# Block sums of weights formed by accumulating loads in a two-layer trunk kernel, with first pairs of a block loaded ahead

## The chip, the cores and the metric

The kernel runs on one core of a Trainium2 chip. The metric is the device time of one execution in microseconds, the median over several runs; lower is better. One execution was profiled by the hardware profiler, and the rows quoted below come from its trace.

## The reference, cut to what matters

Two residual layers act on x (512 tokens, 1024 features). Layer 0 mixes by a gated short convolution and a gated linear recurrence, layer 1 by stick-breaking attention; each is followed by a squared-ReLU MLP with 4096 hidden features, which is where the change lies. All modulation vectors come from `c_act @ ada_w[layer]`.

```python
for layer in range(2):
    mod = c_act @ ada_w[layer] + ada_b[layer]          # ada_w: (2, 1024, 6144)
    shift1, scale1, gate1, shift2, scale2, gate2 = split(mod, 6)
    h = rms_norm(x, norm_mix[layer]) * (1 + scale1) + shift1
    x = x + gate1 * mixer(h)
    h = rms_norm(x, norm_mlp[layer]) * (1 + scale2) + shift2
    x = x + gate2 * (square(relu(h @ mlp_w1[layer])) @ mlp_w2[layer])
```

## The kernel before

**Precision.** Each product of float32 matrices is made from three matmuls (`mm3`, L278): the high part of the weight times the high and the low part of the data, and the low part of the weight times the high part of the data. A weight tile of 128 x 1024 is loaded by SyncE's queue into a ring of three raw buffers (`raw_w`, L258), ScalarE casts it to its high part (`whi`, L271), VectorE subtracts that to get the low part (`wlo`, L272), into rings of four (`split_w`). Hidden tiles are split in the same way (`split`, L288; low parts at L291).

**The MLP** (`mlp`, L1127) makes the 32 hidden tiles of 128 features in four blocks of eight. After each block the second weight matrix is applied to it: outputs o = 0 to 7, eight k steps of 3 matmuls of 512 columns each, added onto x by `x_add` (L506). Block 3 does five outputs there and leaves the last three to the next stage.

**Pairs.** Most hidden tiles are made two at a time, as a 2 x 2 block product of halves (the weights A11, A12 of one tile and A21, A22 of the other; the data's halves of features and of tokens) with seven products of half size instead of eight (Winograd's form of Strassen's scheme), each of 4 k steps x 3 matmuls = 12 matmuls of 256 columns. `pair_w` (L1047) makes the left-hand sums on VectorE into `tt`, which has four places of 1024 columns: S1 = A21 + A22 (L1058), S2 = S1 − A11 (L1059), S4 = A12 − S2 (L1061), S3 = A11 − A21 (L1062). The splits are wa (A11, A12), wb (S1, S2), wc (S4, S3) and wd (A22). `pair` (L1068) runs the products in the order wa, wb, wb, wa, wc, wc, wd; the last, `last()`, runs behind the first products of the next pair. `sums` (L1007) makes the right-hand sums t0 to t3 (high and low parts) once for each layer, from the normalised tiles of h that also stand in `tt`; so `tt` is free for the first pair's sums only after the last low part (L1021) is made. Each raw load of 512 KB goes by SyncE; there are 13 pairs in each layer: pair 3 of block 0 and four in each of blocks 1 to 3.

**Block 0** differs: its first four tiles are made as a head (`mlp_head`, L1177 for layer 0; L1657 to L1672 for layer 1) in two halves of tokens, by k steps, as h becomes ready, each half with four psum banks; tiles 4 and 5 are then made whole (`whole_tile`, L1117), and tiles 6 and 7 are pair 3.

**Background.** In layer 0 `background(2)` after each output of blocks 0 to 2 issues two loads of the ada weights of layer 1 (48 in these blocks), through the same ring of raw buffers and the same queue; VectorE makes their dot products with c (L420).

**Order.** In the MLP only TensorE's order is as written by hand. The orders of SyncE, ScalarE, VectorE and GpSimd follow from the order of emission in the program, through the tile scheduler. The head of layer 1 is placed by a planner (`Graph`), which has costs and due times for its steps and TensorE's order as given. GpSimd has hardly any work in the kernel.

Of the kernel before, what the change touches and what calls it, by code (L numbers as in the profile page):

```python
# [23 lines left out]
P = 128  # L24
# [196 lines left out]
def trunk(tc, x_d, c_d, rep_d, small_d, const_d, ada_d, ws_d, win_d, wv_d, woab_d, w1_d, w2_d, wqk_d, wvc_d, woc_d, out_d):  # L221
# [63 lines left out]
    def ks(k):  # L285
        return slice(k * P, (k + 1) * P)
# [720 lines left out]
    def sums(l, th, on):  # L1007


        lo_, hi_ = slice(0, 4), slice(4, 8)  # L1010
        q = lambda k, hf: tt3[:, k, H[hf]]
        regs = lambda k, hf: [(i, hf) for i in range(k.start, k.stop)]
        s2, hd = l * 48 + SHIFT2 * 8, Handle()
        on("DVE", 8, lambda: dve.tensor_tensor(dsh[:, 4 * l:4 * l + 4], modc[:, s2 + 4:s2 + 8], modc[:, s2:s2 + 4], op=ALU.subtract), [], [hd])
        view = lambda t_: t_.rearrange("p (k t) -> p k t", t=256)

        def high(i, k, hf):
            on("ACT", 1024, lambda: act.copy(view(th[i][0].t), q(k, hf)), regs(k, hf), [th[i][0]])

        def low(i, k, hf):  # L1020
            on("DVE", 1024, lambda: dve.tensor_tensor(view(th[i][1].t), q(k, hf), view(th[i][0].t).bitcast(F32), op=ALU.subtract),  # L1021
               regs(k, hf) + [th[i][0]], [th[i][1]])
# [24 lines left out]
    def pair_w(l, i, hp):  # L1047


        r0, r1 = raw_w(w1_d[l, 2 * i]), raw_w(w1_d[l, 2 * i + 1])  # L1050
        a, b = slice(0, T), slice(T, 2 * T)

        def place():
            nsum[0] += 1
            n = (nsum[0] - 1) % 4
            return tt[:, 1024 * n:1024 * n + 1024]
        wa, s_ = split_w(r0, None, AT256), place()
        dve.tensor_tensor(s_[:, a], r1[:, a], r1[:, b], op=ALU.add)  # L1058
        dve.tensor_tensor(s_[:, b], s_[:, a], r0[:, a], op=ALU.subtract)  # L1059
        wb, z_ = split_w(s_, None, AT256), place()  # L1060
        dve.tensor_tensor(z_[:, a], r0[:, b], s_[:, b], op=ALU.subtract)  # L1061
        dve.tensor_tensor(z_[:, b], r0[:, a], r1[:, a], op=ALU.subtract)  # L1062
        wc = split_w(z_, None, AT256)
        wd = [hp.tile([P, 576], F32R, name=n, tag=n)[:, 16:528] for n in ("wdh", "wdl")]
        split(r1[:, b], *wd)
        return wa, wb, wc, wd

    def pair(l, i, hp, th, hid, before):  # L1068


        wa, wb, wc, wd = pair_w(l, i, hp)
        a, b, c = [acc(256) for _ in range(3)]
        cm = [hp.tile([P, T], F32, name="cm", tag="cm", bufs=3) for _ in range(2)]
        out = [hid_new(hp, 2 * i + j) for j in range(2)]
# [14 lines left out]

        def relu2(j, sl, ps=None):  # L1090
            c_ = cm[j][:, sl]
            act.activation(c_, c_ if ps is None else ps, AF.Relu)
            act.activation(c_, c_, AF.Square)
            split(cm[j], *out[j], sl)

# [18 lines left out]
            relu2(1, H[0], a)  # L1114
        return last

    def whole_tile(l, j, hp, hid):  # L1117

        w, ps, c_ = load_w(w1_d[l, j]), acc(), hp.tile([P, T], F32, name="cm", tag="cm", bufs=3)
# [4 lines left out]
        act.activation(c_, c_, AF.Square)  # L1124
        split(c_, *hid[j])

    def mlp(l, last, hp, head, th):  # L1127
# [49 lines left out]
    def mlp_head(l, nin, hp):  # L1177
# [2 lines left out]
        later(TN, lambda: nin.finish(acc(256), 1))  # L1180
        hid = [hid_new(hp, j) for j in range(4)]

        def head(hf):
            ps = [acc(256) for _ in range(4)]
            for k in range(NT):
                for j in range(4):
                    mm3(ps[j], w[j], ks(k), hT[k], H[hf], k == 0, k == NT - 1)
                yield 1.28
            for j in range(4):
                c_ = hp.tile([P, T], F32, name="cm", tag="cm", bufs=3)  # L1190
                act.activation(c_[:, H[hf]], ps[j], AF.Relu)
                act.activation(c_[:, H[hf]], c_[:, H[hf]], AF.Square)
                split(c_, *hid[j], H[hf])

        run(head(0))
# [136 lines left out]
    def mm3h(ps, cut, w, wc, hs_, hs, start, stop, n, **kw):  # L1332

        h = hs_[0]
        def fn():
            mm3(cut(ps.t), (w[0].t, w[1].t), wc, (h[0].t, h[1].t), hs, start, stop)
        return on_pe(3 * (n * 0.000417 + 0.002), fn, w + tuple(a for h_ in hs_ for a in h_), (ps,), 1, **kw)


# [316 lines left out]

    w = [weights(w1_d[1, j], None, AT256) for j in range(4)]  # L1657
    for hf, sl in enumerate(H):
        ps = [r.new() for r in (accs, accs, zts, miscs)]
        for k, j in by_half(hf, 4):  # L1660
            order.append(mm3h(ps[j], half, w[j], ks(k), (hh[hf][k],), sl, k == 0, k == NT - 1, 256))
        for j in range(4):
            c_, (hi, lo) = cms.new(), hid[j]
            on_act(256, lambda c_=c_, p_=ps[j], sl=sl: act.activation(c_.t[:, sl], half(p_.t), AF.Relu), (ps[j],), (c_,), 0, psum=True)
# [91 lines left out]
```

## Time and profile before

| what | value |
|---|---|
| median of 3 runs | 1263.33 us (fastest 1261.52; a third run of 2425.68 lies far off) |
| profiled execution | 1267.05 us |
| its span in the trace | 1265.3 us |
| granted clock of TensorE, mean | 0.985 |
| DMA | 163.50 MB, mean 129 GB/s |

In the rows below, PE is TensorE's matmuls, PEld its weight loads, DVE VectorE, ACT ScalarE, POOL GpSimd, SP SyncE (SPq its DMA queue). L281 is line 281 of the kernel. In a matmul `b` is the psum bank. A wait row names the engine and line that waited, what it waited for, the total in microseconds, the number of times and the longest. A group row ends with busy time, mean nanoseconds of one, idle time ahead and what ended it. In a DMA row stand the queue, the count, the KB of each and the median time from issue to landing.

### The profile page before, as it was taken

The numbers are of one execution on the slowest core, as the hardware profiler recorded it, in microseconds if no ns is written. First come the engines' busy times: TensorE is split into PE (matmuls) and PEld (weight loads), VectorE is DVE, ScalarE is ACT, GpSimd is POOL, SyncE is SP. The second block draws the span as 40 slices with busy tenths as digits, with TensorE's granted clock in tenths as the row PEclk, the third lists the DMA queues.
The fourth block names the chain that finished last, engine by engine and source line by source line (L and its number), as shares of the span: only waits on it lengthen the run. The fifth ranks groups of instructions, "written<-read, shape, count | busy, mean of one in ns | idle before, by whom it ended". The sixth has DMA issues, their size and how long they took to land.

```text
span 1265.3 us, 19233 instructions
## 1 busy us (share of the span) xinstructions
PE 1227.5 (97%) x7649; PEld 1066.8 (84%) x7649; DVE 891.7 (70%) x1435; ACT 616.7 (49%) x1111; POOL 13.8 (1%) x24
## 2 busy tenths in 40 slices
PE   7999999989999989999999999999989999999998
PEld 6888777888889889889978787778888898898998
DVE  8997777658788687786567764668786574675661
ACT  4433133337338247157357763667565274372560
POOL 0000000000000000000030000000000000000000
PEclk8999899999999989999999999999999999999999
DMA  8666454312764745744312212231113323143141
GB/s 305 252 209 213 161 167 133 133 35 64 250 203 135 253 145 171 253 143 134 107 53 92 84 51 83 85 100 68 51 50 101 100 87 131 67 149 102 51 151 50
DMA packets 46618, 163.50 MB, mean 129 GB/s; under 512 B 5296, under 2 KB 6328, under 8 KB 46528
## 3 DMA queue, kind: packets, MB, share of 16 engines
q1 hardware_dynamic: 46384, 161.78, 38.5%
q8 instruction: 60, 0.98, 0.3%
q10 hardware_dynamic: 144, 0.49, 0.1%
q14 instruction: 30, 0.25, 0.1%
HBM read 155.96 MB, written 2.10 MB: 125 GB/s over the span
## 4 chain that ended last, share of the span: by engine, by line
PE 73%; DVE 10%; DMA 10%; ACT 4%; issue 2%; SPq 0%; ACTq 0%; DVEq 0%
PE b L281 16%; PE b L283 16%; PE b L282 16%; DMA wraw<-in_w 6%; DVE wlo L272 4%; DMA wraw<-in_ada 3%; PE acc L281 3%; PE acc L283 3%; PE acc L282 3%; ACT whi L271 2%; PE acc L652 2%; PE b L1495 1%; PE b L1516 1%; PE b L1551 1%; PE b L1415 1%
## 5 line engine op out<-in xcount | busy, mean ns | idle before, releaser
L271 ACT CAST whi<-wraw 128x1024 fp32r<-128x1024 f32 x125 | 129.7, 1048 | 243.1 <-DMA wraw<-in_w 102.5
L282 PE MATMUL b<-hidl,whi 128*128 128x512 f32 (+1 forms) x560 | 208.3, 372 | 1.5 <-DVE hidl L291 1.5
L281 PE MATMUL b<-hidh,whi 128*128 128x512 f32 (+1 forms) x560 | 208.4, 372 | 0.0
L283 PE MATMUL b<-hidh,wlo 128*128 128x512 f32 (+1 forms) x560 | 207.8, 371 | 0.0
L281 PE MATMUL b<-hh,whi 128*128 128x256 f32 (+1 forms) x632 | 197.7, 313 | 7.0 <-DVE x L506 6.3
L272 DVE TENSOR_TENSOR wlo<-wraw,whi 128x1024 fp32r<-128x1024 f32 x125 | 152.1, 1222 | 62.9 <-ACT whi L271 61.4
L283 PE MATMUL b<-hh,wlo 128*128 128x256 f32 (+1 forms) x632 | 193.2, 306 | 2.3 <-DVE wlo L272 2.3
L282 PE MATMUL b<-hl,whi 128*128 128x256 f32 (+1 forms) x632 | 192.8, 305 | 0.0
L281 PEld LDWEIGHTS b<-hh,whi 128*128 128x128 f32 x632 | 121.1, 192 | 20.1 <-issue 7.2
L506 DVE SCALAR_TENSOR_TENSOR x<-b,modc,x 128x512 f32<-128x512 f32 (+1 forms) x102 | 68.1, 675 | 88.6 <-PE b L283 88.5
L283 PEld LDWEIGHTS b<-hh,wlo 128*128 128x128 f32 x632 | 120.7, 191 | 8.6 <-DVE wlo L272 3.2
L282 PEld LDWEIGHTS b<-hl,whi 128*128 128x128 f32 x632 | 121.3, 192 | 4.5
L282 PEld LDWEIGHTS b<-hidl,whi 128*128 128x128 f32 x560 | 105.5, 188 | 20.7 <-DVE hidl L291 2.8
L283 PEld LDWEIGHTS b<-hidh,wlo 128*128 128x128 f32 x560 | 105.1, 188 | 18.5
L281 PEld LDWEIGHTS b<-hidh,whi 128*128 128x128 f32 x560 | 105.1, 188 | 18.3
L420 DVE CUSTOM_DVE_ANT_0 ascr<-wraw,cb 128x1024 bf16<-128x1024 f32 x80 | 97.8, 1222 | 31.0 <-DMA wraw<-in_ada 30.8
L272 DVE TENSOR_TENSOR wlo<-tt,whi 128x1024 fp32r<-128x1024 f32 x52 | 63.5, 1222 | 19.7 <-ACT whi L271 19.0
L271 ACT CAST whi<-tt 128x1024 fp32r<-128x1024 f32 x52 | 53.2, 1049 | 41.5 <-PE b L282 25.3
L291 DVE TENSOR_TENSOR hidl<-cm,hidh 128x256 fp32r<-128x256 f32 (+1 forms) x90 | 44.5, 510 | 20.1 <-ACT hidh L290 19.3
L1329 DVE TENSOR_TENSOR wlo<-raw,whi 128x1024 fp32r<-128x1024 f32 x34 | 41.5, 1221 | 21.9 <-ACT whi L1328 21.6
L281 PE MATMUL acc<-hh,whi 128*128 128x512 f32 x128 | 52.9, 414 | 0.0
L1479 DVE TENSOR_TENSOR_SCAN om<-om,pat 128x772 f32<-128x772 f32 (+2 forms) x24 | 46.5, 1936 | 5.8 <-ACT om L1475 5.8
(378 smaller groups left out, 2654.2 us busy)
## 6 DMA issues: line engine op xcount, KB each, us to landing
wraw<-in_w SPq DMA_DIRECT2D x124, 512.0 KB, 3.6
wraw<-in_ada SPq DMA_DIRECT2D x80, 512.0 KB, 4.3
eraw<-in_ada SPq DMA_DIRECT2D x16, 512.0 KB, 3.8
wraw<-in_win SPq DMA_DIRECT2D x16, 512.0 KB, 4.1
raw<-in_wqk SPq DMA_DIRECT2D x16, 512.0 KB, 3.7
raw<-in_ws SPq DMA_DIRECT2D x8, 512.0 KB, 6.0
wraw<-in_woab SPq DMA_DIRECT2D x8, 512.0 KB, 3.3
raw<-in_wvc SPq DMA_DIRECT2D x8, 512.0 KB, 3.2
```

The costliest lines, as they stand in the source:

```text
L271: act.copy(hi, raw)
L272: dve.tensor_tensor(lo, raw, hi.bitcast(F32), op=ALU.subtract)
L281: pe.matmul(ps, whi, h[0][:, hs], start=start, stop=False, **kw)
L282: pe.matmul(ps, whi, h[1][:, hs], start=False, stop=False, **kw)
L283: pe.matmul(ps, wlo, h[0][:, hs], start=False, stop=stop, **kw)
L291: dve.tensor_tensor(lo[:, sl], t_[:, sl], hi[:, sl].bitcast(F32), op=ALU.subtract)
L420: dve.tensor_tensor_reduce(out=scr, in0=raw, in1=cb, scale=1.0, scalar=0.0, op0=ALU.mult, op1=ALU.add, accum_out=modr[:, col:col + 1])
L506: dve.scalar_tensor_tensor(x[o][:, sl], ps, mcol(l, v, o), x[o][:, sl], op0=ALU.mult, op1=ALU.add)
L652: order.append(on("PE", 8 * 0.000417 * (sl.stop - sl.start), lambda k=k, wi=wi, hi_=hi_, sl=sl, w=w: [pe.matmul(sacc[j][:, sl], w[wi].t[:, ...
L1329: on_dve(1024, lambda: dve.tensor_tensor(lo.t, raw.t, hi.t.bitcast(F32), op=ALU.subtract), (raw, hi), (lo,), 1)
L1415: on_pe(0.13, lambda s=s, sq=sqs[p, s, s0]: pe.matmul(ms.t[64 + 32 * s:96 + 32 * s, sl], hs, sq.t[:, sl], start=True, stop=True), (sqs[p, ...
L1479: on_dve(2 * nw, lambda: dve.tensor_tensor_scan(s_(), s_(), pats[i][:, ::-1], 0.0, op0=ALU.mult, op1=ALU.max), (om,), (om,), 2)
```

## The change

The signs are chosen so that each left-hand sum is an addition. Two of the four are then formed by a load of one operand by SyncE into `tt`, and a second load, of the other operand, by GpSimd's queue with `accum_op=add` onto the first (which must wait until the first has landed): S1 = A21 + A22 as before, and S3' = A21 + A11. VectorE keeps S2' = S1 + A11 and S4' = A12 + S2'. A22 is loaded once more by itself for wd (256 KB). The operands' signs are carried by a scale of ±1 in the casts and subtractions of the right-hand sums, and row 2 of the pair, which comes out negated, by a scale of −1 in its first ReLU. A pair's loads are now four by SyncE (512, 256, 256 and 256 KB) and two by GpSimd (256 KB each), 1.75 MB in place of 1 MB in two loads.

Beside that:

- `pair_w` is a generator in three steps. In blocks 0 to 2, when output 6 is reached, output 7's weights and the first two steps of the next block's first pair (wa, wb) are emitted ahead of output 6's products, and the third step (wc, wd) ahead of output 7's.
- Background loads stand in `PIECES`: 14, 12, 12 and 10 in blocks 0 to 3, all behind outputs 0 to 4, instead of 16, 16, 16 and none behind outputs 0 to 7.
- In the head of layer 0 the first half of tokens uses two banks, each for two tiles, and the second half is made tile by tile; the weights of tiles 4 and 5 are loaded behind the first two of these, and the right-hand sums are emitted behind the second. The head of layer 1 uses two banks for the first half and four others for the second.

```diff
     def sums(l, th, on):
...
         def high(i, k, hf):
-            on("ACT", 1024, lambda: act.copy(view(th[i][0].t), q(k, hf)), regs(k, hf), [th[i][0]])
+            on("ACT", 1024, lambda: act.activation(view(th[i][0].t), q(k, hf), AF.Copy, scale=1.0 if i == 2 else -1.0), regs(k, hf), [th[i][0]])
 
         def low(i, k, hf):
-            on("DVE", 1024, lambda: dve.tensor_tensor(view(th[i][1].t), q(k, hf), view(th[i][0].t).bitcast(F32), op=ALU.subtract),
-               regs(k, hf) + [th[i][0]], [th[i][1]])
+            on("DVE", 1024, lambda: dve.scalar_tensor_tensor(view(th[i][1].t), q(k, hf), 1.0 if i == 2 else -1.0,
+               view(th[i][0].t).bitcast(F32), op0=ALU.mult, op1=ALU.subtract), regs(k, hf) + [th[i][0]], [th[i][1]])
...
     def pair_w(l, i, hp):
-        r0, r1 = raw_w(w1_d[l, 2 * i]), raw_w(w1_d[l, 2 * i + 1])
         a, b = slice(0, T), slice(T, 2 * T)
+        a11, a21, a22 = w1_d[l, 2 * i][:, a], w1_d[l, 2 * i + 1][:, a], w1_d[l, 2 * i + 1][:, b]
...
-        wa, s_ = split_w(r0, None, AT256), place()
-        dve.tensor_tensor(s_[:, a], r1[:, a], r1[:, b], op=ALU.add)
-        dve.tensor_tensor(s_[:, b], s_[:, a], r0[:, a], op=ALU.subtract)
-        wb, z_ = split_w(s_, None, AT256), place()
-        dve.tensor_tensor(z_[:, a], r0[:, b], s_[:, b], op=ALU.subtract)
-        dve.tensor_tensor(z_[:, b], r0[:, a], r1[:, a], op=ALU.subtract)
-        wc = split_w(z_, None, AT256)
-        wd = [hp.tile([P, 576], F32R, name=n, tag=n)[:, 16:528] for n in ("wdh", "wdl")]
-        split(r1[:, b], *wd)
-        return wa, wb, wc, wd
-
-    def pair(l, i, hp, th, hid, before):
-        wa, wb, wc, wd = pair_w(l, i, hp)
+        def added(out, one, other):
+            sync.dma_start(out, one)
+            pool_e.dma_start(out, other, accum_op=ALU.add)
+        r0 = raw_w(w1_d[l, 2 * i])
+        s_ = place()
+        added(s_[:, a], a21, a22)
+        w = [split_w(r0, None, AT256)]
+        yield w
+        z_ = place()
+        added(z_[:, b], a21, a11)
+        dve.tensor_tensor(s_[:, b], s_[:, a], r0[:, a], op=ALU.add)
+        w.append(split_w(s_, None, AT256))
+        yield w
+        dve.tensor_tensor(z_[:, a], r0[:, b], s_[:, b], op=ALU.add)
+        r1 = wp.tile([P, 1024], F32, name="wraw", tag="raw", bufs=3)[:, :T]
+        sync.dma_start(r1, a22)
+        w.append(split_w(z_, None, AT256))
+        w.append([hp.tile([P, 576], F32R, name=n, tag=n)[:, 16:528] for n in ("wdh", "wdl")])
+        split(r1, *w[3])
+        yield w
+
+    def pair(i, hp, th, hid, before, steps_):
+        for w in steps_:
+            pass
+        wa, wb, wc, wd = w
...
-            act.activation(c_, c_ if ps is None else ps, AF.Relu)
+            act.activation(c_, c_ if ps is None else ps, AF.Relu, scale=1.0 - 2 * j)
...
+    PIECES = ((3, 3, 3, 3, 2), (3, 3, 2, 2, 2), (3, 3, 2, 2, 2), (2, 2, 2, 2, 2))
...
+    def mlp(l, last, hp, head, th, more=()):
...
-                for j in (4, 5):
-                    whole_tile(l, j, hp, hid)
+                for n, j in enumerate((4, 5)):
+                    whole_tile(more[n] if more else load_w(w1_d[l, j]), j, hp, hid)
             for i in range(len(hid) // 2, 4):
-                rest = pair(l, 4 * b + i, hp, th, hid, rest)
+                rest = pair(4 * b + i, hp, th, hid, rest, ahead or pair_w(l, 4 * b + i, hp))
+                ahead = None
...
-                if b < 3:
-                    background(2)
+                if o < 5:
+                    background(PIECES[b][o])
...
             for o in range(2, n):
-                p = second(o)
+                p = p1 if o == n - 1 and b < 3 else second(o)
+                if o == n - 2 and b < 3:
+
+                    p1, ahead = second(n - 1), pair_w(l, 4 * b + 4, hp)
+                    next(ahead)
+                    next(ahead)
                 products(p, 0, 8)
                 done(o, p[0])
+                if o == n - 2 and b < 3:
+                    w = next(ahead)
+                    ahead = [w]
...
-        def head(hf):
-            ps = [acc(256) for _ in range(4)]
...
+        def first():
+            ps = [acc() for _ in range(2)]
+            ps = [ps[j // 2][:, H[j % 2]] for j in range(4)]
             for k in range(NT):
                 for j in range(4):
-                    mm3(ps[j], w[j], ks(k), hT[k], H[hf], k == 0, k == NT - 1)
+                    mm3(ps[j], w[j], ks(k), hT[k], H[0], k == 0 and j % 2 == 0, k == NT - 1, skip_group_check=True)
                 yield 1.28
...
+        def second(j):
+            ps = acc(256)
+            for k in range(NT):
+                mm3(ps, w[j], ks(k), hT[k], H[1], k == 0, k == NT - 1)
+                yield 0.32
+            evict(j, ps, H[1])
+
+        run(first())
         flush()
-        th = [[Handle(t=hp.tile([P, 1088], F32R, name=f"t{i}{a}", tag=f"t{i}{a}")[:, AT512]) for a in "hl"] for i in range(4)]
-        sums(l, th, lambda eng, n, fn, r, w: fn())
-        run(head(1))
-        return hid, [(a.t, b.t) for a, b in th]
+        more = []
+        for j in range(4):
+            run(second(j))
+            if j < 2:
+                more.append(load_w(w1_d[l, 4 + j]))
+            if j == 1:
+                th = [[Handle(t=hp.tile([P, 1088], F32R, name=f"t{i}{a}", tag=f"t{i}{a}")[:, AT512]) for a in "hl"] for i in range(4)]
+                sums(l, th, lambda eng, n, fn, r, w: fn())
+        return hid, [(a.t, b.t) for a, b in th], more
...
     w = [weights(w1_d[1, j], None, AT256) for j in range(4)]
     for hf, sl in enumerate(H):
-        ps = [r.new() for r in (accs, accs, zts, miscs)]
+        ps = [accs.new() for _ in range(2)] if hf == 0 else [zts.new() for _ in range(4)]
+        ps = [(ps[j // 2], lambda t_, j=j: t_[:, H[j % 2]]) if hf == 0 else (ps[j], half) for j in range(4)]
```

More of the change, by code (lines that the diff above doesn't have):

```diff
@@ L1115, in pair, with whole_tile @@
         return last
-    def whole_tile(l, j, hp, hid):
-        w, ps, c_ = load_w(w1_d[l, j]), acc(), hp.tile([P, T], F32, name="cm", tag="cm", bufs=3)
+    def whole_tile(w, j, hp, hid):
+        ps, c_ = acc(), hp.tile([P, T], F32, name="cm", tag="cm", bufs=3)
         for k in range(NT):
@@ L1132, in mlp @@
             if b == 0:
[L1133 to L1134 removed]
+                for n, j in enumerate((4, 5)):
+                    whole_tile(more[n] if more else load_w(w1_d[l, j]), j, hp, hid)
             for i in range(len(hid) // 2, 4):
[L1136 removed]
+                rest = pair(4 * b + i, hp, th, hid, rest, ahead or pair_w(l, 4 * b + i, hp))
+                ahead = None
             n = 8 if b < 3 else 5
@@ L1181, in mlp_head, with evict @@
         hid = [hid_new(hp, j) for j in range(4)]
-        def head(hf):
-            ps = [acc(256) for _ in range(4)]
+        def evict(j, ps, sl):
+            c_ = hp.tile([P, T], F32, name="cm", tag="cm", bufs=3)
+            act.activation(c_[:, sl], ps, AF.Relu)
+            act.activation(c_[:, sl], c_[:, sl], AF.Square)
+            split(c_, *hid[j], sl)
+        def first():
+            ps = [acc() for _ in range(2)]
+            ps = [ps[j // 2][:, H[j % 2]] for j in range(4)]
             for k in range(NT):
                 for j in range(4):
-                    mm3(ps[j], w[j], ks(k), hT[k], H[hf], k == 0, k == NT - 1)
+                    mm3(ps[j], w[j], ks(k), hT[k], H[0], k == 0 and j % 2 == 0, k == NT - 1, skip_group_check=True)
                 yield 1.28
             for j in range(4):
[L1190 to L1195, printed above, removed]
-        flush()
-        th = [[Handle(t=hp.tile([P, 1088], F32R, name=f"t{i}{a}", tag=f"t{i}{a}")[:, AT512]) for a in "hl"] for i in range(4)]
-        sums(l, th, lambda eng, n, fn, r, w: fn())
-        run(head(1))
-        return hid, [(a.t, b.t) for a, b in th]
+                evict(j, ps[j], H[0])
+        def second(j):
[5 more added lines that the diff above has]
+        run(first())
+        flush()
+        more = []
[7 more added lines that the diff above has]
+        return hid, [(a.t, b.t) for a, b in th], more
     m_s = ExitStack()
@@ L1335, in fn @@
         def fn():
-            mm3(cut(ps.t), (w[0].t, w[1].t), wc, (h[0].t, h[1].t), hs, start, stop)
+            mm3(cut(ps.t), (w[0].t, w[1].t), wc, (h[0].t, h[1].t), hs, start, stop, skip_group_check=True)
         return on_pe(3 * (n * 0.000417 + 0.002), fn, w + tuple(a for h_ in hs_ for a in h_), (ps,), 1, **kw)
@@ L1658, in trunk @@
     for hf, sl in enumerate(H):
-        ps = [r.new() for r in (accs, accs, zts, miscs)]
+        ps = [accs.new() for _ in range(2)] if hf == 0 else [zts.new() for _ in range(4)]
+        ps = [(ps[j // 2], lambda t_, j=j: t_[:, H[j % 2]]) if hf == 0 else (ps[j], half) for j in range(4)]
         for k, j in by_half(hf, 4):
-            order.append(mm3h(ps[j], half, w[j], ks(k), (hh[hf][k],), sl, k == 0, k == NT - 1, 256))
+            order.append(mm3h(*ps[j], w[j], ks(k), (hh[hf][k],), sl, k == 0 and (hf == 1 or j % 2 == 0), k == NT - 1, 256))
         for j in range(4):
-            c_, (hi, lo) = cms.new(), hid[j]
-            on_act(256, lambda c_=c_, p_=ps[j], sl=sl: act.activation(c_.t[:, sl], half(p_.t), AF.Relu), (ps[j],), (c_,), 0, psum=True)
+            c_, (hi, lo), (p_, cut) = cms.new(), hid[j], ps[j]
+            on_act(256, lambda c_=c_, p_=p_, cut=cut, sl=sl: act.activation(c_.t[:, sl], cut(p_.t), AF.Relu), (p_,), (c_,), 0, psum=True)
             on_act(256, lambda c_=c_, sl=sl: act.activation(c_.t[:, sl], c_.t[:, sl], AF.Square), (c_,), (c_,), 0)
```

1 line of the change is left out of this document (removed).

## The prediction

> **What bounds the kernel now.** I read the page's busy shares first, then the windows of like stages in the two layers against each other, then the waits of TensorE in the stretch where the windows differ.
>
> ```profile
> PE 1227.5 (97%) x7649; PEld 1066.8 (84%) x7649; DVE 891.7 (70%) x1435; ACT 616.7 (49%) x1111; POOL 13.8 (1%) x24
> ```
>
> TensorE is busy for 97% of the span, so only time that it waits, or runs at half clock after a wait, can be won; VectorE has 30% to spare. The windows (columns: microseconds, then busy time and count of PE, PEld, DVE, ACT, POOL, granted clock, DMA share, GB/s) show where. The first three rows are the four-pair stages that open blocks 1 to 3 of layer 0, the fourth is the same work in layer 1:
>
> ```profile
> 368.10:407.90 39.80, 38.08 (x326) 37.23 (x326) 35.92 (x55) 29.25 (x55) 0.00 (x0) 1.00 0.37 124
> 453.60:498.70 45.10, 41.69 (x326) 41.08 (x325) 39.01 (x59) 30.08 (x57) 0.00 (x0) 0.92 0.35 121
> 544.40:586.80 42.40, 39.25 (x326) 38.64 (x325) 37.73 (x57) 30.93 (x58) 0.00 (x0) 0.96 0.33 114
> 1011.20:1049.40 38.20, 38.20 (x326) 38.19 (x325) 29.26 (x44) 29.14 (x55) 0.00 (x0) 1.00 0.29 99
> 301.10:313.20 12.10, 12.10 (x46) 9.87 (x47) 8.79 (x14) 7.86 (x13) 0.00 (x0) 0.86 0.35 107
> 946.70:957.60 10.90, 10.90 (x51) 9.01 (x50) 10.65 (x15) 6.72 (x13) 0.00 (x0) 1.00 0.37 109
> ```
>
> In layer 1 PE is busy for 38.20 of 38.20 us, with DVE at 29.26: nothing to win there. In layer 0 the same stages take 39.8, 45.1 and 42.4, together 12.7 us more than three times 38.2. The last two rows are whole tiles 4 and 5 of block 0 in layer 0 and in layer 1: 12.1 against 10.9, at a clock of 0.86. The waits of PE in layer 0's MLP say what it stood for:
>
> ```profile
> PE b L281 <- ACT whi L271: 4.7, 3, 2.2
> PE b L283 <- DVE wlo L272: 4.6, 6, 1.7
> PE b L281 <- DVE x L506: 3.2, 1, 3.2
> PE b L282 <- DVE hidl L291: 1.5, 3, 1.1
> ```
>
> Weights that come late head the list; then one wait for the banks of the last x_add (the head), and one for hidden tiles, which this change leaves alone.
>
> **The change, part by part.**
>
> **(1) First pairs prepared ahead.** The timeline row (start, duration, instruction, wait) of the second product of a block's first pair:
>
> ```profile
> 458.07 0.38 PE L281 MATMUL b<-t0h,whi 128*128 128x256 f32 x1 [2.20 <-ACT whi L271]
> 1040.88 0.28 PE L281 MATMUL b<-t0h,whi 128*128 128x256 f32 x1
> ```
>
> Layer 0 waits 2.2 us for wb, whose sums queue on DVE behind the background's dot products; layer 1 doesn't wait. Emitting the loads and splits of wa and wb before output 6's products gives them two outputs, 11 us, of lead. I book all **−12.7**: the clock loss in it has no other cause. What wc and wd need comes before output 7's products, 5.5 us plus two products ahead.
>
> **(2) Whole tiles loaded inside the head.** Wait and slow clock go together:
>
> ```profile
> 301.09 0.50 PE L283 MATMUL b<-hh,wlo 128*128 128x512 f32 x1 [1.67 <-DVE wlo L272]
> ```
>
> 1.67 plus 12.1 − 10.9 = **−2.9**. The loads move ahead of the sums, and the sums after two of four columns.
>
> **(3) Head by two banks.** The first half needs two free banks where four were needed, so the 3.2 us for x_add goes. But the fourth weight's low half is late next, in both layers:
>
> ```profile
> 273.95 1.21 DVE L272 TENSOR_TENSOR wlo<-wraw,whi 128x1024 fp32r<-128x1024 f32 x1
> 922.61 1.22 DVE L1329 TENSOR_TENSOR wlo<-raw,whi 128x1024 fp32r<-128x1024 f32 x1
> ```
>
> The head started at 274.08, and this operand lands at 275.16; in layer 1 at 923.83. The wait only changes its name. I book three short matmuls brought forward, 3 x 0.116 in each layer: **−0.7** (a product of 12 takes 1.39, the time between the start of a pair, 957.60 above, and its second product, 958.99 below). Bounds: 0, and all 3.2 in each, −6.4.
>
> **(4) Background loads bunched.** Before, two ada loads follow each of eight outputs; afterwards all stand behind outputs 0 to 4. Output 5's weight load thus has 14 ada loads of its block ahead of it in block 0, and 12 in blocks 1 and 2, where it had 10. The queue in these stages:
>
> ```profile
> wraw<-in_ada SPq DMA_DIRECT2D x13, 512.0 KB, 4.5
> wraw<-in_w SPq DMA_DIRECT2D x9, 512.0 KB, 4.3
> ```
>
> ```profile
> 407.90:453.60 45.70, 45.47 (x206) 37.38 (x205) 31.85 (x51) 11.48 (x16) 0.00 (x0) 1.00 0.77 254
> ```
>
> 22 loads in 45.7 us through a ring of three buffers are 2.08 each; so output 5's load comes 4 x 2.08 = 8.3 later in block 0 and 4.2 in blocks 1 and 2. Output 5 starts three outputs of (45.7 − 1.4)/8 = 5.54 before the stage's end: 453.6 − 16.6 = 437.0, and at 351.5 in block 0 (which ends where the next stage starts, 368.1); its low half is wanted two matmuls of 0.23 later. It was ready at the ends of these:
>
> ```profile
> 434.13 1.22 DVE L272 TENSOR_TENSOR wlo<-wraw,whi 128x1024 fp32r<-128x1024 f32 x1 [2.25 <-ACT whi L271]
> 346.74 1.23 DVE L272 TENSOR_TENSOR wlo<-wraw,whi 128x1024 fp32r<-128x1024 f32 x1 [1.03 <-ACT whi L271]
> ```
>
> Slack is 437.45 − 435.35 = 2.1 and 351.95 − 347.97 = 4.0. New waits: 2.1 in block 1, the same taken for block 2, and 4.3 in block 0: **+8.5**. Bounds: 0, where the ring was fed late by its consumers and not by its loads, and +16.6, the shift with no slack.
>
> Block 3 carries ten ada loads that it hadn't; its stage has the room that blocks 0 to 2 lose (48 either way).
>
> In the row at 301.09 a wait of 1.67 us was followed by a stage at clock 0.86, so each of these waits may cost 1.2 more; I leave these 3.6 in the range. The Trainium skill's page "TensorE: Matmul & The Clock Gate", section "What's actually happening", has the clock drop after an idle window of about 3.4 us; by that only the 4.3 could cost clock. The row with 1.67 disagrees, and the measurement decides.
>
> **(5) Sums by a second load.** Each of 26 pairs loses two subtractions or additions on DVE:
>
> ```profile
> L1058 DVE TENSOR_TENSOR tt<-wraw 128x512 f32<-128x512 f32 x12 | 8.2, 686 | 0.9 <-DMA wraw<-in_w 0.8
> ```
>
> 52 x 0.69 = 36 us of DVE, worth nothing by itself, since PE in layer 1 waits for none of it. The signs moved into relu's scale and into the sums' casts and subtractions go into instructions that exist: nothing. The loads grow from 1 to 1.75 MB a pair; DMA is at 0.29 to 0.37 in these stages, so bytes aren't the limit. Delay is: S1 is no longer load, 0.69, but load, then POOL's wait for its landing, then a second transfer, in series, of a kind of which no trace here has one. Call that A, from the end of POOL's wait to landing. Bounds from rows of 256 KB:
>
> ```profile
> stq<-stq SPq DMA_DIRECT2D x16, 256.0 KB, 3.4
> ...
> x<-in_x SPq DMA_DIRECT2D x8, 256.0 KB, 4.1
> ...
> out_y<-x SPq DMA_DIRECT2D x5, 256.0 KB, 2.0
> ```
>
> At least 2.0; at most the two slow ones in series, 7.5, since it reads both operands. I take **5**, near the middle, the nearest row being a plain load at 4.1; a plain 256 KB load I take as 3.0, between 2.0 and 4.1.
>
> The Trainium skill's page "DMA: Bandwidth & Descriptors", section "Anatomy of one DMA — SWDGE (gpsimd) path", gives some 2.0 us plus bytes at 436 GB/s, an estimate of 2.6 for A; no run here shows it. By it the waits of the next paragraph vanish and the time would be about 1255.5; by my 5 they stay.
>
> Where it bites first is pair 3 of block 0, whose places in tt are still read by the last right-hand sums:
>
> ```profile
> 948.14 1.22 DVE L1021 TENSOR_TENSOR t2l<-tt,t2h 128x1024 fp32r<-128x1024 f32 x1
> 958.99 0.28 PE L281 MATMUL b<-t0h,whi 128*128 128x256 f32 x1
> ```
>
> ```profile
> 297.55 1.22 DVE L1021 TENSOR_TENSOR t2l<-tt,t2h 128x1024 fp32r<-128x1024 f32 x1
> ```
>
> Free at 949.36, then 3.0 + 5 + 0.69 + cast 1.05 + subtraction 1.22 = 960.3; wanted two matmuls after 958.99, 959.2: wait 1.1. In layer 0 the sums come one column (24 x 0.116 = 2.8) later, free at about 301.8, so 312.8, wanted 301.09 − 1.67 + 10.9 + 1.39 + 0.24 = 312.0: wait 0.8. Together **+1.9**; at A = 2.0 nothing, at 7.5 +6.9.
>
> The steady pairs: SP's next loads wait on z_a as now, and there the loop is one pair long.
>
> ```profile
> SPq L260 <- DVE tt L1061: 20.0, 2, 10.7
> ```
>
> ```profile
> 1024.59 1.11 SPq L260 DMA_DIRECT2D wraw<-in_w  x2
> ```
>
> The loop is 3.0 + A + 2 x 0.69 = 4.4 + A, against 7 x 1.39 = 9.7 of products: no slip up to A = 5.3. The lead is 1040.88 − 1024.59 = 16.3, less load, addition, cast and subtraction 10.6 is left for A. At 5: **0**.
>
> **Sum.** −12.7 − 2.9 − 0.7 + 8.5 + 1.9 = −5.9. The profiled execution took 1267.05 us, span 1265.3, so 1261.1 on its scale; the median of the runs is 1263.3, 3.7 below it, so the forecast is **1257.4**. Own range: bunching free and A short gives 1247; A at 7 costs 2 x 2 at pair 3 and (below) 9 in the steady pairs, with a clock loss or two: 1274.
>
> **Rivals.**
>
> **Slower: the accumulating load is late in every pair.** Over three pairs of a block the loop slips 3(A − 5.3) and the spare lead is 10.6 − A: it decides from A = 6.6. Price at A = 8: 3 x 2.7 − 2.6 = 5.5 for each of six four-pair blocks, 33; 2 x 3 at pair 3; and 18 waits near 1.7 may cost 1.2 of clock each, 21.6. That is 1296 to 1318, 1307 in the middle. For it: two landings in series on a path SP shares, and the 9 to 11 us that SP already stands on z_a. Against: 16.3 us of lead. The Trainium skill's same page, "Rules for kernel authors", has the accumulating form on GpSimd alone and waiting for the earlier transfer's semaphore, which speaks for it; no run here shows its length.
>
> **Faster: bunching costs nothing.** The three ada loads behind the early outputs may find the ring idle for some of the time, so −13.5 or so: 1249; with the heads' waits gone as well, 1244. For it: DMA at 0.77, not 1. Against: ACT and DVE must finish each buffer before its reuse, and 2.08 is a mean over the whole stage.
>
> **No gain at the first pairs.** If wb still comes late, its chain longer by A, half of 12.7 is lost, and the plan's shifts take the rest: 1264. For it: `ahead` sits behind the outputs whose loads part 4 delays. Against: 11 us of lead.
>
> That the change doesn't do what it says, DVE being no freer because its split waits for the sum's landing, would look like the first rival.
>
> **How the numbers follow.** Forecast 0.52; slower 0.17 (1307); faster 0.17 (1244 to 1249); no gain 0.14. Two per cent, about what a measurement of this kernel can tell from no change, is 25.3 us: 1238.1 and 1288.6. Nearly all of the first rival lies above, and a little of the forecast's tail: slower 0.18. Below 1238 needs the second rival and more: 0.06. Same 0.76. The range 1240 to 1290 takes in the forecast, the faster and the no-gain case and leaves out most of the slower one.
>
> **What would show it.** Right: no PE wait for whi in the first pairs of blocks 1 to 3, each stage near 38.2 at clock 1.00; tiles 4 and 5 in 10.9; a new wait of 2 to 4 us at output 5 of blocks 0 to 2; a wait near 1 at pair 3's wb; the head's 3.2 now on wlo; no wait in layer 1's steady pairs; the POOL queue's landing at 5 or so. Wrong: waits on whi or tt behind POOL in each pair of layer 1, or DVE's z_a standing for the accumulating load; or PE idle at another place of layer 0 by over 10 us.

## The result and the profile after

The changed kernel takes **1303.57 us** (median of 5 runs, 1297.94 to 1305.15); the kernel before takes 1263.33 in the same comparison. The ratio is **1.0292**, 95% interval 1.0264 to 1.0321. By the medians the change costs 40 us, by the ratio 37; 1257.4 was forecast and 1290 was the end of the range. The profiled execution has a span of 1296.2 us, 30.9 above that of before. It was the fastest of the five, and the stretch ahead of the MLP of layer 0, which the change leaves alone, happens to be 3.8 us shorter in this trace (266.1 against 269.9).

The busy shares on the page, then the waits of TensorE in layer 0's MLP and in layer 1's (columns: total, times, longest):

```profile
PE 1235.5 (95%) x7649; PEld 1067.1 (82%) x7649; DVE 866.0 (67%) x1383; ACT 616.4 (48%) x1111; POOL 59.0 (5%) x76
```

```profile
PE b L282 <- DVE hidl L291: 8.0, 3, 3.8
PE b L281 <- ACT whi L271: 6.4, 4, 3.2
PE b L283 <- DVE wlo L272: 4.0, 7, 0.8
PE b L281 <- DVE x L506: 2.9, 1, 2.9
PE b L1408 <- DVE nss L1398: 2.7, 1, 2.7
```

```profile
PE b L281 <- ACT whi L271: 5.7, 1, 5.7
PE b L1408 <- DVE nss L1398: 4.6, 1, 4.6
PE b L283 <- DVE wlo L272: 2.2, 3, 1.0
PE b L281 <- ACT hidh L290: 1.3, 1, 1.3
PE b L281 <- ACT kept L1101: 1.2, 3, 0.4
PE b L282 <- DVE hidl L291: 0.8, 1, 0.8
```

VectorE is busy for 25.7 us less (891.7 to 866.0), and TensorE does the same 7649 matmuls in a longer time. Layer 1's MLP, where nothing waited once the head was through, now waits for a pair's sums (whi, wlo) and for hidden tiles (hidh, hidl). The largest single waits stand at the first sums of pair 3 in each layer:

```profile
309.80 0.39 PE L281 MATMUL b<-t0h,whi 128*128 128x256 f32 x1 [3.15 <-ACT whi L271]
```

```profile
978.25 0.58 PE L281 MATMUL b<-t0h,whi 128*128 128x256 f32 x1 [5.67 <-ACT whi L271]
```

The windows of whole tiles 4 and 5 of layer 0, of the three four-pair stages of layer 0 (each found by the same matmuls as before) and of the same stage of layer 1:

```profile
294.15:305.05 10.90, 10.90 (x50) 9.03 (x49) 7.13 (x11) 6.06 (x12) 2.77 (x3) 1.00 0.62 185
376.36:416.25 39.89, 38.41 (x326) 37.77 (x325) 25.69 (x39) 27.21 (x53) 6.15 (x7) 1.00 0.60 153
465.47:503.36 37.89, 37.89 (x326) 37.69 (x325) 25.45 (x36) 27.22 (x53) 6.12 (x7) 1.00 0.65 165
555.79:595.33 39.54, 38.36 (x326) 37.76 (x325) 27.42 (x40) 27.17 (x53) 2.60 (x3) 1.00 0.44 120
1033.47:1072.03 38.56, 38.16 (x326) 37.75 (x325) 26.06 (x38) 28.64 (x55) 6.11 (x7) 1.00 0.61 158
```

The tiles take the 10.9 that was booked, at clock 1.00. Of the block-opening stages of layer 0, the first is as long as before (39.89 against 39.80) and the other two are shorter; in the first and the third TensorE stands idle for 1.5 and 1.2. DMA's share has gone from 0.29 to 0.61 in layer 1's stage. The DMA rows of that stage say more. Before (queue, count, KB, median us from issue to landing), and then after:

```profile
wraw<-in_w SPq DMA_DIRECT2D x8, 512.0 KB, 3.4
```

```profile
wraw<-in_w SPq DMA_DIRECT2D x6, 512.0 KB, 5.3
tt<-in_w POOLq DMA_DIRECT2D x7, 256.0 KB, 6.2
tt<-in_w SPq DMA_DIRECT2D x6, 256.0 KB, 2.8
```

An accumulating load of 256 KB takes 6.2 us in the median of this stage, and the plain loads of whole weight tiles, which aren't part of any sum, take 5.3 where they took 3.4. How an accumulation behaves alone and in company is seen in two short windows of the same trace:

```profile
tt<-in_w SPq DMA_DIRECT2D x1, 256.0 KB, 2.8
tt<-in_w POOLq DMA_DIRECT2D x1, 256.0 KB, 3.7
```

```profile
wraw<-in_w SPq DMA_DIRECT2D x2, 512.0 KB, 6.0
tt<-in_w POOLq DMA_DIRECT2D x2, 256.0 KB, 8.8
```

At 1116 one has the engines to itself and lands after 3.7. At 1147 two start 0.6 us apart, beside two plain loads, and take 8.8 in the median (8.2 and 9.4), the loads 6.0.

The Trainium skill's page "DMA: Bandwidth & Descriptors", section "Queues, rings and completion order", says that each DMA engine takes packets in turn from the queues that have work for it. The trace agrees as far as it goes: plain loads on SP's queue are stretched from 3.4 to 5.3 while GpSimd's queue is busy.

Whoever waits on such a load holds up what stands behind it on its engine. ScalarE at the end of that stage (start, duration, instruction, wait), and TensorE after it:

```profile
1075.91 1.04 ACT L271 CAST whi<-wraw 128x1024 fp32r<-128x1024 f32 x1 [3.00 <-DMA wraw<-in_w]
1076.86 0.61 ACT L290 CAST hidh<-cm 128x512 fp32r<-128x512 f32 x1
```

```profile
1077.53 0.50 PE L281 MATMUL b<-hidh,whi 128*128 128x512 f32 x1 [1.26 <-ACT hidh L290]
```

The cast of a second-matrix weight, whose load is late, stands ahead of the cast of a hidden tile that TensorE needs now. The waits for `hidl`, 8.0 us in layer 0, are of this kind too: VectorE stood at dot products whose ada loads were late, with the hidden chain behind them. The longest of the three:

```profile
323.45 1.22 DVE L420 CUSTOM_DVE_ANT_0 ascr<-wraw,cb 128x1024 bf16<-128x1024 f32 x1 [3.62 <-DMA wraw<-in_ada]
...
324.61 0.42 DVE L1124 TENSOR_TENSOR cm<-b,kept 128x256 f32<-128x256 f32 x1
326.13 1.23 DVE L420 CUSTOM_DVE_ANT_0 ascr<-wraw,cb 128x1024 bf16<-128x1024 f32 x1 [1.10 <-DMA wraw<-in_ada]
...
327.28 1.02 DVE L291 TENSOR_TENSOR hidl<-cm,hidh 128x512 fp32r<-128x512 f32 x2
```

Since TensorE runs the same 7649 matmuls in the same order in every version, each stage can be measured from its first matmul to the first of the next (the last to the end of the span). Summed over both layers, in us, from one trace of each; the last two columns are experiments that the next section describes:

| stages | before | changed | DVE sums | plain second load |
|---|---|---|---|---|
| pair 3 of block 0 (2) | 17.0 | 32.0 | 17.0 | 28.8 |
| four-pair stages (6) | 241.7 | 236.3 | 229.0 | 229.4 |
| outputs of a block (8) | 369.0 | 398.5 | 380.4 | 381.4 |

Against DVE sums the changed kernel loses 15.0, 7.4 and 18.1 us: most in the outputs, whose weights are no pair's sums.

### The profile page after: what moved, and what is told of

Read it like the earlier page. It is cut to its first block, busy times and chain, and to the rows that moved or that the text cites. A ratio compares the mean times of both kernels' runs of the same rounds, so it can differ in the third digit from the quotient of the medians.

```text
span 1296.2 us, 19439 instructions
## 1 busy us (share of the span) xinstructions
PE 1235.5 (95%) x7649; PEld 1067.1 (82%) x7649; DVE 866.0 (67%) x1383; ACT 616.4 (48%) x1111; POOL 59.0 (5%) x76
## 4 chain that ended last, share of the span: by engine, by line
PE 64%; DVE 14%; DMA 12%; ACT 7%; issue 3%; SPq 0%; DVEq 0%; ACTq 0%; POOLq 0%
PE b L281 14%; PE b L283 14%; PE b L282 14%; DMA wraw<-in_w 5%; DVE wlo L272 4%; PE acc L281 3%; ACT whi L271 3%; PE acc L283 3%; PE acc L282 3%; DMA wraw<-in_ada 2%; DVE ascr L420 2%; DMA raw<-in_ws 2%; PE b L1541 1%; PE b L1562 1%; DMA tt<-in_w 1%
## 5 line engine op out<-in xcount | busy, mean ns | idle before, releaser
L282 PE MATMUL b<-hidl,whi 128*128 128x512 f32 (+1 forms) x560 | 211.4, 377 | 8.9 <-DVE hidl L291 8.8
L281 PE MATMUL b<-hidh,whi 128*128 128x512 f32 (+1 forms) x560 | 212.2, 379 | 4.6 <-ACT whi L271 3.2
L283 PE MATMUL b<-hidh,wlo 128*128 128x512 f32 (+1 forms) x560 | 210.7, 376 | 2.1 <-DVE wlo L272 2.1
L1061 POOL DMA_DIRECT2D tt<-in_w x52 | 45.6, 910 | 881.1 <-DMA tt<-in_w 409.9
L1107 ACT ACTIVATE cm<-cm 128x512 f32<-128x512 f32 (+1 forms) x52 | 27.0, 521 | 62.9 <-DVE cm L1121 57.9
```

What stands on the lines that cost most here:

```text
L281: pe.matmul(ps, whi, h[0][:, hs], start=start, stop=False, **kw)
L282: pe.matmul(ps, whi, h[1][:, hs], start=False, stop=False, **kw)
L283: pe.matmul(ps, wlo, h[0][:, hs], start=False, stop=stop, **kw)
L1061: pool_e.dma_start(out, other, accum_op=ALU.add)
L1107: act.activation(c_, c_ if ps is None else ps, AF.Relu, scale=1.0 - 2 * j)
```

## The experiments

Theory A: the accumulating loads are the loss, by their own length and by slowing loads beside them. Theory B: the moved background loads and the new order are the loss. Ratios are to the kernel before, run beside each on the same chip; 0.001 is 1.27 us. Each version is scheduled anew, so a difference between two of them also holds what the new order of the engines other than TensorE does.

**DVE sums** (all sums on VectorE, everything else of the change kept).

```diff
-        added(s_[:, a], a21, a22)
...
-        added(z_[:, b], a21, a11)
...
+        dve.tensor_tensor(s_[:, a], r1[:, a], r1[:, b], op=ALU.add)
+        dve.tensor_tensor(z_[:, b], r1[:, a], r0[:, a], op=ALU.add)
```

> All four sums of a pair on DVE again, from two plain 512 KB loads, with the new signs; the early first pairs, the bunched background and the new heads stay. Theory A (the accumulating loads are the loss, by their own length and by slowing other loads beside them): 1252 to 1262 us, no wait of PE at the first product from t0 in pair 3, and the waits of bunching (about 6) and of the norm's statistics in block 3 (about 4.6) remain. Theory B (the moved background loads and the new order are the loss, the accumulating loads are hidden): 1290 or more.

Measured: 1259.72 us against 1266.33, ratio **0.9949** (0.9925 to 0.9974). Theory A holds, theory B falls. The four-pair stages of this run, in the order of the four rows of before:

```profile
368.79:407.02 38.23, 38.23 (x326) 38.19 (x326) 29.64 (x45) 27.75 (x54) 0.00 (x0) 1.00 0.31 107
453.95:492.14 38.19, 38.19 (x326) 38.18 (x325) 29.76 (x46) 27.67 (x54) 0.00 (x0) 1.00 0.33 107
538.77:576.94 38.17, 38.17 (x326) 38.17 (x325) 29.94 (x46) 27.82 (x54) 0.00 (x0) 1.00 0.32 108
1007.55:1045.75 38.20, 38.20 (x326) 38.19 (x325) 29.25 (x44) 29.16 (x55) 0.00 (x0) 1.00 0.29 99
```

Each is full. 127.3 − (38.23 + 38.19 + 38.17) = 12.7: the first pairs' gain came to the tenth of a microsecond, so long as no accumulation is in the way. What TensorE still waits for in layer 0:

```profile
PE b L281 <- ACT whi L271: 3.1, 3, 2.0
PE b L283 <- DVE wlo L272: 2.9, 6, 0.5
PE b L281 <- DVE x L506: 2.9, 1, 2.9
PE b L1403 <- DVE nss L1393: 2.7, 1, 2.7
```

The first two rows, 6.0, are the bunched background. The fourth, the norm's statistics behind the ten dot products of block 3, hadn't been foreseen.

**Accumulating loads alone** (the kernel before, with `pair_w`, the signs in `sums` and in `relu2`, and nothing else of the change).

> The kernel before with the accumulating loads and the signs alone: no early first pairs, background two behind each of eight outputs, old heads. Theory A: 1285 to 1300 us, with waits at the first sums of pair 3 in both layers and late in the four-pair stages of layer 1. Theory B: 1263 to 1268.

Measured: 1304.17, ratio **1.0297** (1.0281 to 1.0313), a little over the top of theory A's figure. With the accumulating loads in the kernel, the rest of the change is worth nothing on balance (1.0292 with it, 1.0297 without); without them it is worth half a per cent. By place it does something: the six four-pair stages take 258.1 us here and 236.3 in the changed kernel, but the outputs 382.4 and 398.5, and pair 3 25.4 and 32.0.

**Background back** (`background(2)` behind each output of blocks 0 to 2, the rest as changed).

> The changed kernel with two background loads behind each of eight outputs in blocks 0 to 2 and none in block 3. Theory A: 1288 to 1296 us (the changed kernel's 1303.6 less about 6 of waits at outputs 3 and 4 and less about 4.6 at the norm's statistics). Theory B: about 1265.

Measured: 1300.5, ratio 1.0262 (1.0234 to 1.0290). Theory B is out again. The 11 us expected aren't seen: 1.0292 − 1.0262 is 4 us, within what the two intervals leave open.

**Plain second load** (GpSimd's load overwrites; the sums S1 and S3' are then A22 and A11 alone).

```diff
-            pool_e.dma_start(out, other, accum_op=ALU.add)
+            pool_e.dma_start(out, other)
```

> GpSimd's second load overwrites where it added: the sums are then one operand alone, and everything else (bytes, queue, wait for the first landing) stays. If the addition in the transfer is what is long: from POOL's issue to landing 3.5 us or less in the median where the changed kernel has 5.8, and the time falls by 10 us or more, to 1293 or less. If the second transfer in series on that queue and the traffic are what is long: 5 to 6 us, and the time stays within 5 us of 1303.6.

Measured: 1275.66, ratio **1.0086** (1.0054 to 1.0117). The row over the whole run:

```profile
tt<-in_w POOLq DMA_DIRECT2D x52, 256.0 KB, 3.8
```

3.8 instead of 5.8 at the same bytes, queue and waits, and 1.0292 − 1.0086 = 0.0206, 26 us, are gone. It is the addition in the transfer that costs most. The pages' rows for GpSimd's queue (packets, MB, share of the time of 16 engines) show what goes with it, changed kernel first:

```profile
q0 software_dynamic: 7488, 13.63, 6.5%
```

```profile
q0 software_dynamic: 4160, 13.63, 3.1%
```

For the same bytes the accumulating loads make 144 packets each instead of 80, and their packets occupy each of the 16 engines for some 1.6 us a load (6.5% of 1296.2 / 52) instead of 0.8. By place the addition costs 17 us in the outputs, 7 in the four-pair stages and 3 at pair 3 (the table above). What the plain second load leaves over DVE sums stands at pair 3, 11.8 of 13.2. The median didn't fall to 3.5 and the time fell by more than 10, so the first branch holds in time and falls short in length.

**Same loads, no accumulation** (A21 into both places and the second tile's row, all by SyncE with no wait between, VectorE adds).

```diff
+        sync.dma_start(s_[:, a], a21)
+        r1 = raw_w(w1_d[l, 2 * i + 1])
...
+        sync.dma_start(z_[:, b], a21)
+        dve.tensor_tensor(s_[:, a], s_[:, a], r1[:, b], op=ALU.add)
+        dve.tensor_tensor(z_[:, b], z_[:, b], r0[:, a], op=ALU.add)
```

> The same extra loads (A21 twice into its places in tt, the second tile's row as well) all by SyncE's queue with no wait between them, 1.5 MB a pair, and DVE adds. If the extra bytes are a good part of the loss: 1270 us or more. If the loss lies in the series of two landings and in the adding transfer: within 6 of the kernel with DVE sums alone, 1256 to 1266.

Measured: 1264.03, ratio 0.9985 (0.9964 to 1.0006). The extra bytes cost 0.0036 over DVE sums, 4.5 us, but the intervals overlap, so this may be nothing. They don't stretch the plain loads either. The same stage of layer 1 in this run, and with the plain second load on GpSimd's queue:

```profile
wraw<-in_w SPq DMA_DIRECT2D x8, 512.0 KB, 3.4
```

```profile
wraw<-in_w SPq DMA_DIRECT2D x6, 512.0 KB, 4.3
```

3.4 with the extra loads on SP's own queue, 4.3 with plain loads on GpSimd's, 5.3 with accumulating ones: part of the stretch comes with the second queue and part with the addition. So the chain of runs splits the loss of 1.0292 − 0.9949 = 0.0343, 43 us: more plain loads 4.5, a second landing in series on GpSimd's queue 0.0101 or 13, the addition in it 26. Each step is a difference of ratios whose intervals are about 0.003 wide on either side, and the run with all loads by SyncE carries 1.5 MB a pair, not 1.75, so the first two terms are rough. The second also holds an order of the queues at pair 3 (under *Pair 3 by VectorE*).

**One accumulation a pair** (S3' is A21 loaded, A11 added by VectorE).

```diff
-        added(z_[:, b], a21, a11)
+        sync.dma_start(z_[:, b], a21)
+        dve.tensor_tensor(z_[:, b], z_[:, b], r0[:, a], op=ALU.add)
```

> Only S1 is formed by the accumulating load; S3' is A21 loaded and A11 added by DVE. If the accumulating loads are long because two run at once: from POOL's issue to landing near 3.8 us in the median (5.8 with two), the loop of load, accumulation and two additions then fits in a pair's 9.7 us, no waits in the four-pair stages of layer 1, and only pair 3 of block 0 late: 1268 to 1280 us. If the length belongs to each by itself: median above 5 and 1290 or more.

Measured: 1278.44, ratio 1.0095 (1.0060 to 1.0129). This lies in the range expected. Half of the accumulations gone takes 25 of 43 us with them; most of what is left stands at pair 3 (12.2 over DVE sums) and in the outputs of layer 0 (7.7). Over the whole run, and TensorE's waits in layer 1:

```profile
tt<-in_w POOLq DMA_DIRECT2D x26, 256.0 KB, 4.3
```

```profile
PE b L281 <- ACT whi L271: 3.8, 1, 3.8
PE b L283 <- DVE wlo L272: 0.5, 1, 0.5
PE b L281 <- ACT kept L1102: 0.4, 1, 0.4
```

A lone accumulation is shorter (4.3 against 5.8), if not the 3.8 expected; layer 1 keeps only the wait at pair 3.

**Pair 3 by VectorE** (`if i == 3`: the DVE sums; 24 pairs as changed).

> The changed kernel with pair 3 of block 0 formed by DVE from two loads in both layers, the other 24 pairs by accumulating loads. If the first sums behind the reads of tt cost what the stages show (3.3 + 0.9 + 2.8 in layer 0, 8.8 in layer 1): 14 to 16 us less than the changed kernel, 1287 to 1291. If they only take up a delay that then comes elsewhere: 1297 or more.

Measured: 1285.3, ratio 1.0148 (1.0114 to 1.0181), 18 us less than the changed kernel, where 14 to 16 were expected. So two pairs of 26 carry two fifths of the loss. The table above has 15.0 at pair 3 itself. There four accumulations, those of two pairs, are queued at once. In layer 1:

```profile
967.57 0.88 POOL L1061 DMA_DIRECT2D tt<-in_w  x1 [310.97 <-ACT cm L1139]
968.68 0.87 POOL L1061 DMA_DIRECT2D tt<-in_w  x1 [0.23 <-issue]
970.74 0.86 POOL L1061 DMA_DIRECT2D tt<-in_w  x1 [1.19 <-DMA tt<-in_w]
974.07 0.86 POOL L1061 DMA_DIRECT2D tt<-in_w  x1 [2.47 <-issue]
```

```profile
976.42 0.69 DVE L1069 TENSOR_TENSOR tt<-tt,wraw 128x512 f32<-128x512 f32 x1 [8.02 <-DMA tt<-in_w]
```

These rows are the changed kernel's. By the semaphores in the trace the addition that makes pair 3's S2', at 976.42, waits for the third of the four, and the first two belong to the next block's first pair, whose S2' is made only here:

```profile
1008.38 0.69 DVE L1069 TENSOR_TENSOR tt<-tt,wraw 128x512 f32<-128x512 f32 x1
```

The next block's loads by SyncE start at 963.98, right behind the end of `t2l` (963.91), and pair 3's at 965.08, right behind that of `t3l` (965.05), whose place in `tt` is free later; GpSimd issues the four one after another. In layer 0 pair 3 has the first two of the four. From pair 3's first load at 965.08 to the landing of its accumulation at 976.33 are 11.3 us, where the forecast's 3.0 + 5 made 8, and its places come free 5.0 after the start of the whole tiles, where the trace of before has 2.7. The forecast's chain has the high part of wb 0.1 late; 0.1 + 3.3 + 2.3 make up the wait of 5.67. What the order of the two pairs is worth by itself wasn't measured. TensorE's wait is followed by slow clock, the last column but two:

```profile
978.25:981.65 3.40, 2.94 (x12) 2.64 (x13) 2.96 (x3) 2.80 (x5) 0.00 (x0) 0.50 0.65 197
```

3.4 us at 0.50 are 1.7 more.

**Accumulations apart** (S3' emitted behind S4').

> The changed kernel with the accumulating load of S3' emitted behind S4' rather than ahead of S2'. If two accumulating loads in flight together are what stretches them: median from POOL's issue to landing falls from 5.8 towards 3.8 and the time by 10 to 20 us, 1284 to 1294, unless S3' is then late for wc. If they stay in flight together (the scheduler still issues them one behind the other): 5 to 6 us and within 5 of 1303.6.

Measured: 1300.89, ratio 1.0278 (1.0237 to 1.0318), median 5.5. The emission alone didn't move them apart: GpSimd still issues the two of a pair 0.6 to 1.9 us after each other in 20 of 26 pairs (19 in the changed kernel). The run tells nothing for or against the stretching.

**All sums on VectorE, background back.**

> All sums on DVE and the background two behind each of eight outputs again: the early first pairs and the new heads alone are left of the change. From the run with DVE sums (3.6 us below the kernel before in its stages), less the waits at outputs 3 to 5 (6.3 and about 2) and at the norm's statistics of block 3 (5.4): 1248 to 1253 us on the scale where the kernel before has 1263. If the bunched background is what lets the first pairs come early, they lose part of their 14 us again: 1256 to 1262.

Measured: 1257.21, ratio 0.9937 (0.9913 to 0.9961), by the ratio 1255: short of the first figure. The second case is what the trace shows, for the first pair of block 2 waits again:

```profile
451.07 0.39 PE L281 MATMUL b<-t1h,whi 128*128 128x256 f32 x1 [2.94 <-ACT kept L1096]
```

TensorE waits here for ScalarE to empty a bank. By stages of layer 0, against DVE sums, the outputs are 12.6 us shorter (183.1 for 195.7) and the four-pair stages 9.3 longer (123.8 for 114.5): bunching the background has a price, but it is also what clears ScalarE and VectorE for the early first pairs. With DVE sums alone and with this the ratios can't be told apart.

**All sums on VectorE, 12 background loads in each block.**

```diff
-    PIECES = ((3, 3, 3, 3, 2), (3, 3, 2, 2, 2), (3, 3, 2, 2, 2), (2, 2, 2, 2, 2))
+    PIECES = ((3, 3, 2, 2, 2), (3, 3, 2, 2, 2), (3, 3, 2, 2, 2), (3, 3, 3, 3, 0))
```

> All sums on DVE, the early first pairs and the new heads, and 12 background loads in each block (3, 3, 2, 2, 2 in blocks 0 to 2; 3, 3, 3, 3, 0 in block 3). The run with DVE sums lost 6.3 us behind the 14 loads of block 0 and 5.4 at the norm's statistics of block 3. If those go with the number of loads and with the place of the last ones: about 4 less in block 0 and 3 to 5 less in block 3, ratio to the kernel before 0.989 (1250 to 1255 us). If neither moves: 0.995, as with DVE sums.

Measured: 1258.31, ratio 0.9945 (0.9926 to 0.9965): in the time no step beyond DVE sums. In its trace block 0 waits for no weight of its outputs any more and the wait at the statistics is 0.5 instead of 2.7, but block 3 waits 2.6 for its weights. The two places moved as the first case has it; the time, with its interval, doesn't decide.

**The same with the old head of layer 1.**

> The same with the old head of layer 1 (four banks for each half). The new head cost 1.05 us in each run that had it: 1 us less than the run beside it, 0.001, below what the comparison can tell; in the trace the step of about 1 at that place goes.

Measured: 1259.84, ratio 0.9961 (0.9940 to 0.9981). Expected was a gain of 0.001; no gain is seen, and the intervals leave the sign open.

The four versions with DVE sums and early first pairs, without extra loads, beat both kernels, the one before by 0.4 to 0.6 per cent (each interval ends below 1), and can't be ranked among themselves.

## Why the prediction was wrong, point by point

**(5) is the step that failed: "I take 5, near the middle, the nearest row being a plain load at 4.1", and from it "At 5: 0" for the steady pairs and +1.9 at pair 3.** The whole run gives a median of 5.8, but no single figure would have done. Alone an accumulation takes 3.7, below the 5; where two are in flight they take up to 9.4, and nine of the 52 exceed the upper bound of 7.5; and 19 of the 26 pairs issue their two within 1.8 us. The sum priced one A by itself in a chain, and took "bytes aren't the limit" from a DMA share of 0.29 to 0.37. It left out that the second accumulation shares the engines with the first, and that both stretch the loads beside them (3.4 to 5.3). Booked for the accumulating loads: +1.9; measured: 1.0292 − 0.9949, 43 us. By place, against DVE sums: 15.0 at pair 3, booked at 1.9; 7.4 in the four-pair stages, booked at 0; and 18.1 in the outputs, for which the sum had no term.

The Trainium skill's estimate for A, 2.6 by "DMA: Bandwidth & Descriptors", section "Anatomy of one DMA — SWDGE (gpsimd) path", stands near the shortest plain loads on that queue (2.75 at the least, 3.8 in the median of that run) and below every accumulating one, the shortest of which took 3.7; the measurement decides.

**Pair 3** was named as the place where it bites first, and the form of the chain was right; its size was off, 18 us by the run with that pair on VectorE. Most of it stays with a plain second load (11.8 of 15.0), so here it is two landings in series, with two pairs' loads queued together, more than the addition. In layer 0 the forecast's own terms give 301.6 where it has 301.8, a wait of 0.5 for 0.8; that changes nothing.

**The first rival** gave the time, 1307 for 1303.6, but not quite by its mechanism. It has every four-pair stage slip, at 33 us in all, with 6 at pair 3 and 21.6 of slow clock. The six stages slipped by 7.4 against DVE sums (3.1 of it in the four whose windows are shown), and pair 3 lost 15.0. The largest part, 18.1, stands in the outputs, 14.0 of it in layer 0, where late loads hold up the hidden chain and the weights; no rival named that. There 8.0 of waits for `hidl` stand, where the kernel with DVE sums has none. So its time is partly luck. These lengths hold waits and slow clock together; how much of the outputs' loss is clock, and how much is the last pair's sums, wasn't separated.

**(1) First pairs**: −12.7, as booked, in the run with DVE sums. In the changed kernel the stages give 127.3 − 117.3 = 10.0 of it.

**(2) Whole tiles**: the wait of 1.67 at 301.09 is gone and the stage takes 10.90. As booked.

**(3) Heads**: booked −0.7, on the ground that the fourth weight's low half is late next. In layer 0 the wait for x remains instead, 2.9 of 3.2; in layer 1 4.6 stand at the statistics, where 3.1 for x and 1.3 for the statistics stood before. No gain, and the new waiter is another one than named.

**(4) Bunching**: booked +8.5 for three waits at output 5. Measured are waits of 6.0 with DVE sums, at outputs 3 to 5; with the slow clock the outputs of blocks 0 to 2 are 7.1 longer than before, 5.0 of it in block 0. The mechanism holds. What it left out is block 3: "its stage has the room" holds for its DMA, but its ten dot products stand on VectorE ahead of the norm's statistics, 2.7 us of wait that weren't booked, and the stage is 4.3 longer.

**All but (5)**: booked −12.7 − 2.9 − 0.7 + 8.5 = −7.8; measured 0.9949, −6.4 with −9.5 to −3.3 as interval. The errors of these terms are small beside that of (5). So one term of the sum, the only one for an operation that the trace of before doesn't show, carried nearly the whole error, and its bounds were built from rows in which no second transfer of the kind was in flight.

## What to carry to other kernels

An operation that no row of the profile shows should be priced with the company that the change itself gives it: two of them at once, beside the loads that run there anyway; not alone. Moving additions from an engine with 30% to spare into the DMA chain exchanges 0.69 us of hidden work for several microseconds of latency in series, and the largest loss came from engines that stood at somebody else's load, with the work that TensorE needed behind it. Where several sums are queued at once, look at which one the queue serves first: the one that is needed next stood behind one needed 32 us later. Where a change has several parts, take each in and out by itself: here a half per cent gain was buried under a three per cent loss.

## What the runs showed of the hardware that had not been expected

An accumulating load of 256 KB by GpSimd takes 3.7 us by itself and a plain load on the same queue 2.75 at its shortest, 3.8 in the median; in company the accumulating one goes up to 9.4. It makes 144 packets where the plain one makes 80, and GpSimd is busy for 0.91 us in the mean to issue it, against 0.54. The plain 512 KB loads beside them go from 3.4 to 5.3 although the 16 DMA engines are busy for only 0.61 of the time in that stage.
